# An fp32 encoder layer on one core: weight sums moved from GpSimd to VectorE at the seams, seven stores moved to GpSimd's queue, and the last output columns scaled ahead

## The chip, the cores and the metric

The kernel runs on one core of one Trainium2 chip. A core has a matrix engine (TensorE, PE in the profile), three engines for element work (VectorE or DVE, ScalarE or ACT, GpSimd or POOL), and SyncE (SP), which here only issues transfers; ACT and GpSimd can issue transfers as well. Each engine runs its own instructions in a fixed order and waits on semaphores for the others. On-chip memory is SBUF (128 partitions) and PSUM (where PE writes); the big tensors lie in device memory. The metric is device microseconds of the execution.

## The reference

Two groups of 512 tokens (prompt and sample, 1024 channels) pass through one layer with shared weights, everything in fp32. What matters here are the parts in which the change lies:

```python
y_m = (sigmoid(o) * hm) @ w_mo                      # mLSTM branch
y_a = mla_attention(...) @ w_ao                     # attention branch
x = x + (g_m * y_m + g_a * y_a) @ w_out
h2 = rmsnorm(x, g_ffn)
x = x + (silu(h2 @ w_gate) * (h2 @ w_up)) @ w_down  # 1024 -> 2816 -> 1024
x = x + sigmoid(x @ w_ple_gate) * (p_l @ w_ple)     # the embedding's rows
return rmsnorm(x, g_final)
```

The last norm divides each token by the root of its mean square over all 1024 channels, and multiplies each channel by its gain. So no output can be finished before the last channel of its tokens is known.

## The kernel before, in words

**Layout.** Activations lie as channels by tokens in tiles of 128x512 (one group's 512 tokens). `x2[g][c]` is the running sum x of group g and channel block c. Group 0 is written first; of group 1 the last two channel blocks are worked in two halves of 256 tokens.

**Three matmuls for one.** Every fp32 operand is split into a rounded part (hi) and a remainder (lo); a product is hi·hi, hi·lo and lo·hi (lines 947, 948 and 949: `xh,wp`, `xl,wp`, `xh,wp`). ACT makes the rounded part with a cast (line 896 for weights, 1229 or 880 for activations), DVE the remainder with a subtraction (line 154). So each weight tile costs ACT one cast and DVE one subtraction, and line 949 is the first matmul of a product that needs the remainder.

**Seven products for eight.** From `w_mo` on, the projections (`mo`, `ao`, then `fg` and `fu` for gate and up, then `down`) are done by a class `Seven`: two column blocks of weights and both token groups form a 2x2 block product, which is done in seven products (P1, P2, P7, P6, P5, Q4, P3) instead of eight. For that, four sums of weight blocks are formed, by `weights` (lines 922, 923, 925, 932: P7 two, P6 one, P3 one), all on GpSimd, and sums of activations, by `Ops.part` (858 P7, 861 P6, 864 P5, 867 Q4). The raw weights of a Seven come as two transfers of 512 KB (384 KB in the third part of down) that ACT issues (line 908), into tiles `wst`, which have two buffers in each of two pools, WP and WX. `outputs` copies PSUM results (982 on ACT, 987 on DVE), and `sg` (line 1199) multiplies gate by up.

**The stages.** `chain` strings the Sevens: mo 0 to 3, ao 0 to 3; then, after the output projection and a norm, eleven pairs of (fg, fu), then 3 x 4 Sevens of down, by parts of 4, 4 and 3 k-blocks. A pair takes the hidden blocks f1 and f2; its seven activation tiles (four products and three or four sums of them, lines 1204 to 1207) are stored to device memory (`actd`, line 1210) through SP's queue and loaded back by down (`ld`, line 828, on SP too). The last pair is the one with f2 = NF - 1; its tiles are read by down's third part only.

**The end.** `halves` loads the weights of the embedding's gate, `proj2` multiplies, and `embed` (DVE twice, ACT once) adds the gated embedding rows (`ld` from `emd`) to x; ACT squares the result (`sq`), DVE adds the squares, PE sums them over partitions (`ssc`), ten small DVE operations make the inverse root (`rv` to `rw`), PE spreads it over partitions (`rbc`), and `finish` multiplies x, gain and `rbc` (`o`, one DVE operation for each channel block) and stores (line 1319, SP). These last functions show as line 79 in the profile where they are called in a fixed order.

**What sets the order.** Up to the embedding's last columns a scheduler orders each engine's instructions by its own times for them. From `pinned[0] = True` on, the order of PE, DVE, ACT and GpSimd is the order of the code; SP's is not fixed by it.

## Time and profile before

| | |
|---|---|
| median of three runs | 1896.21 us (1896.04 to 1897.09) |
| the profiled execution | 1895.6 us |
| its span, first to last event | 1893.8 us |
| granted PE clock, mean | 0.991 |
| PE busy | 1848.4 us, 98% of the span |
| DVE busy | 1234.6 us, 65% |
| ACT busy | 883.3 us, 47% |
| GpSimd (POOL) busy | 448.7 us, 24% |

The profile's times are microseconds from the span's start. A timeline row gives start, duration, engine, line, operation, output and inputs, and in square brackets the idle time of the engine before it and what ended it. Rows of the same line that follow one another directly are drawn together (x2, x4); an operation's duration on DVE and ACT overlaps the start of the next by about 0.1 us, so a row of many shows the pitch. The waits view sums idle time by the pair "who waited for whom": us in total, times, longest.

### The profile page before, as it was taken

How to read it: one execution, taken by the hardware profiler on the slowest of the kernel's cores; microseconds unless marked ns; L12 is line 12 of the kernel's file. 1: busy time of each engine (PE TensorE's matmuls, PEld its weight loads, DVE VectorE, ACT ScalarE, POOL GpSimd, SP SyncE). 2: the span in 40 equal slices, each digit the busy share in tenths (PEclk: the TensorE clock that was granted, in tenths of full speed). 3: DMA queues.
4: the chain of work that ended last, by engine and by line, in shares of the span. 5: the costliest groups of instructions: out<-in, count | busy, mean ns of one | idle time of the engine just before them, and what ended most of it. 6: DMA issues, size and time to landing. Idle time of an engine off the chain costs nothing.

```text
span 1893.8 us, 24548 instructions
## 1 busy us (share of the span) xinstructions
PE 1848.4 (98%) x8849; PEld 1537.3 (81%) x8849; DVE 1234.6 (65%) x2159; ACT 883.3 (47%) x1718; POOL 448.7 (24%) x326
## 2 busy tenths in 40 slices
PE   9999999999999999999999998999999999999997
PEld 7888898988887888777877887888888887887886
DVE  6747575836555667975997586444444458878757
ACT  6255465534443666774543354333333344434442
POOL 0000000100000000352330035666466642322100
PEclk9999999999999999999999999999999999999999
DMA  4111101112253222446455241232323346534232
GB/s 165 52 45 35 56 34 62 40 56 73 78 182 116 65 73 93 126 150 209 153 191 192 95 161 51 91 131 92 103 89 111 112 146 228 165 126 135 90 124 89
DMA packets 98458, 207.59 MB, mean 110 GB/s; under 512 B 10721, under 2 KB 21345, under 8 KB 98337
## 3 DMA queue, kind: packets, MB, share of 16 engines
q1 hardware_dynamic: 86240, 163.03, 25.7%
q10 hardware_dynamic: 12096, 43.00, 7.0%
q8 instruction: 69, 1.13, 0.3%
q14 instruction: 53, 0.43, 0.1%
HBM read 151.89 MB, written 54.10 MB: 109 GB/s over the span
## 4 chain that ended last, share of the span: by engine, by line
PE 84%; DVE 9%; DMA 2%; ACT 2%; issue 2%; SPq 0%; DVEq 0%; ACTq 0%
PE b L947 12%; PE b L949 12%; PE b L948 12%; PE mm L183 8%; PE mm L185 8%; PE mm L184 8%; PE mm L79 4%; PE nm L633 3%; DVE xl L154 2%; PE mm L548 2%; PE mm L550 2%; PE mm L549 2%; DVE wp L154 1%; PE pt L812 1%; PE mm L1296 1%
## 5 line engine op out<-in xcount | busy, mean ns | idle before, releaser
L949 PE MATMUL b<-xh,wp 128*128 128x512 f32 x1148 | 445.1, 393 | 7.5 <-DVE wp L154 7.5
L947 PE MATMUL b<-xh,wp 128*128 128x512 f32 x1148 | 442.5, 394 | 9.4 <-ACT wp L896 3.9
L948 PE MATMUL b<-xl,wp 128*128 128x512 f32 x1148 | 448.9, 392 | 0.0
L896 ACT CAST wp<-wst 128x512 fp32r<-128x512 f32 (+1 forms) x270 | 164.5, 613 | 306.8 <-PE b L949 258.6
L154 DVE TENSOR_TENSOR wp<-wst,wp 128x512 fp32r<-128x512 f32 (+1 forms) x270 | 244.2, 907 | 75.2 <-ACT wp L896 74.9
L947 PEld LDWEIGHTS b<-xh,wp 128*128 128x128 f32 x1148 | 216.5, 189 | 63.0 <-ACT wp L896 8.4
L949 PEld LDWEIGHTS b<-xh,wp 128*128 128x128 f32 x1148 | 216.4, 188 | 56.0 <-DVE wp L154 8.8
L948 PEld LDWEIGHTS b<-xl,wp 128*128 128x128 f32 x1148 | 216.5, 189 | 46.7
L183 PE MATMUL mm<-hh,whi 128*128 128x512 f32 x560 | 220.0, 393 | 0.3 <-ACT raw L79 0.3
L185 PE MATMUL mm<-hh,wlo 128*128 128x512 f32 x560 | 219.5, 392 | 0.0
L184 PE MATMUL mm<-hl,whi 128*128 128x512 f32 x560 | 219.5, 392 | 0.0
L922 POOL TENSOR_TENSOR s<-wst,wst 128x512 f32<-128x512 f32 (+1 forms) x42 | 64.1, 1526 | 422.7 <-DMA wst<-w 268.8
L987 DVE TENSOR_TENSOR u<-b,u 128x512 f32<-128x512 f32 x90 | 61.6, 690 | 142.1 <-PE b L949 85.0
L168 ACT CAST whi<-wst 128x1024 fp32r<-128x1024 f32 (+1 forms) x69 | 71.1, 1030 | 116.5 <-PE mm L184 78.4
L183 PEld LDWEIGHTS mm<-hh,whi 128*128 128x128 f32 x560 | 105.6, 189 | 22.6 <-ACT raw L79 0.8
L185 PEld LDWEIGHTS mm<-hh,wlo 128*128 128x128 f32 x560 | 105.4, 188 | 21.9
L184 PEld LDWEIGHTS mm<-hl,whi 128*128 128x128 f32 x560 | 105.6, 189 | 21.5
L154 DVE TENSOR_TENSOR wlo<-wst,whi 128x1024 fp32r<-128x1024 f32 (+1 forms) x69 | 83.2, 1206 | 30.8 <-ACT whi L168 30.4
L154 DVE TENSOR_TENSOR xl<-ld,xh 128x512 fp32r<-128x512 f32 x121 | 94.1, 806 | 11.3 <-ACT xh L1229 5.9
L982 ACT COPY u<-b 128x512 f32<-128x512 f32 x90 | 50.9, 589 | 107.8 <-PE b L949 80.1
L154 POOL TENSOR_TENSOR vnl<-avt,vnh 128x512 fp32r<-128x512 f32 x16 | 21.2, 1323 | 313.5 <-ACT vnh L158 245.2
L925 POOL TENSOR_TENSOR wst<-wst,wst 128x512 f32<-128x512 f32 (+1 forms) x42 | 79.2, 1886 | 35.9 <-DVE wp L154 33.7
(348 smaller groups left out, 3634.7 us busy)
## 6 DMA issues: line engine op xcount, KB each, us to landing
wst<-w SPq DMA_DIRECT2D x73, 512.0 KB
wst<-w ACTq DMA_DIRECT2D x60, 512.0 KB
ld<-actd SPq DMA_DIRECT2D x77, 256.0 KB
actd<-t SPq DMA_DIRECT2D x44, 256.0 KB
actd<-sg SPq DMA_DIRECT2D x33, 256.0 KB
x<-x SPq DMA_DIRECT2D x32, 256.0 KB
ld<-hzd SPq DMA_DIRECT2D x32, 256.0 KB
wst<-wd ACTq DMA_DIRECT2D x16, 512.0 KB
```

The source lines that it names most:

```text
L79: r = f(*args, **kw)
L154: e.tensor_tensor(out=out, in0=src, in1=hi.bitcast(F32), op=ALU.subtract)
L168: S.copy(hi[:, :n], st[:, :n])
L183: E.matmul(bk, whi[:, c], hi, start=k == 0, stop=False)
L184: E.matmul(bk, whi[:, c], lo, start=False, stop=False)
L185: last_mm[0] = E.matmul(bk, wlo[:, c], hi, start=False, stop=k == nk - 1)
L896: S.copy(hi, src)
L922: GP.tensor_tensor(out=src, in0=a11, in1=a21, op=ALU.add)
L925: GP.tensor_tensor(out=a11, in0=a11, in1=a21, op=ALU.add)
L947: E.matmul(bk, whi[:, c], hi, start=bool(first) and k == 0, stop=False, **sk)
L948: E.matmul(bk, whi[:, c], lo, start=False, stop=False, **sk)
L949: E.matmul(bk, wlo[:, c], hi, start=False, stop=k == self.kh - 1, **sk)
```

## The change

Four edits. `Seven` takes the engine of its weight sums as an argument, and twelve Sevens are given VectorE: the last mo, the first ao, both Sevens of the first and of the last gate pair, and the first and the last of each part of down. That is 48 sums. The Q4 sums of the gate stage's activations (four, line 867) also go to VectorE. The seven stores of the last gate pair are issued by GpSimd; they are the only transfers that GpSimd issues in the program. The embedding's rows are loaded into tiles of the pool's tag `h` (24 buffers) instead of `ev` (8). And at the end the last half's columns of group 1 are multiplied by the gain on ACT ahead of the norm (`scaled`), into three tiles `xg` of the tag `wst` in WP, which has two buffers; DVE then multiplies four, two and two blocks at once by the spread inverse root (`last_out`), and three stores follow, of 512, 256 and 256 KB. The last embedding's step comes one step earlier.

```diff
-        def __init__(self, srcs, kh, ops, out):
+        def __init__(self, srcs, kh, ops, out, adds=None):
+            self.adds = adds or GP
...
-                GP.tensor_tensor(out=src, in0=a11, in1=a21, op=ALU.add)
-                GP.tensor_tensor(out=a21, in0=a21, in1=a22, op=ALU.add)
+                self.adds.tensor_tensor(out=src, in0=a11, in1=a21, op=ALU.add)
+                self.adds.tensor_tensor(out=a21, in0=a21, in1=a22, op=ALU.add)
...
     def pair(kind, c, ops, put):
+        e = V if (kind, c) in (("mo", 3), ("ao", 0)) else GP
...
-    h2 = Ops(hn, lambda: OP("ev", "t"), lambda n: GP if n == "Q4" else V)
+    h2 = Ops(hn, lambda: OP("ev", "t"), lambda n: V)
...
-                    nc.sync.dma_start(actd[f1, n], t_)
+                    (GP if f2 == NF - 1 else nc.sync).dma_start(actd[f1, n], t_)
...
         def make(kind, put):
+            e = V if f1 == 0 or f2 == NF - 1 else GP
...
+                lambda c=c: Seven(
+                    [a[f"wd{pi}"][c], a[f"wd{pi}"][c + 1]], nk, ld, add_to(c, c + 1), V if c in (0, KD - 2) else GP
+                ),
...
-        bp = load(emd[g][c], OP, "ev") if bp is None else bp
+        bp = load(emd[g][c], OP, "h") if bp is None else bp
...
+    def scaled(g, cs, b0, nb):
+        n = nb * P
+        xg = WP("wst", "xg", F32, (P, 1024))[:, 0 : len(cs) * n]
+        for i, c in enumerate(cs):
+            S.activation(
+                out=xg[:, i * n : (i + 1) * n], in_=x2[g][c][:, b0 * P : b0 * P + n], func=AF.Copy,
+                scale=col("g_final", c),
+            )
+        return xg
+
+    def last_out(g, cs, xg, b0, nb):
+        n, k = nb * P, len(cs)
+        tok = slice(b0 * P, b0 * P + n)
+        x3_ = xg.rearrange("p (c t) -> p c t", c=k)
+        V.tensor_tensor(out=x3_, in0=x3_, in1=rs2[g][:, None, :].to_broadcast([P, k, n]), op=ALU.mult)
+        nc.sync.dma_start(a[f"out{g}"][cs[0] : cs[0] + k][:, :, tok].rearrange("c p t -> p c t"), x3_)
...
     first = rs2[1]
+    embed(KD - 1, 1, bk[3], toks[1], bps[1], True)
+    gained = [(cs, scaled(1, cs, H0, H0)) for cs in (range(0, 4), range(4, 6), range(6, 8))]
     finish(1, [0, 1], 0, H0)
-    embed(KD - 1, 1, bk[3], toks[1], bps[1], True)
-    finish(1, [2, 3], 0, H0)
     sums(1, H0, H0)
     inv(1, H0)
-    finish(1, [4, 5], 0, H0)
+    finish(1, [2, 3], 0, H0)
     spread3(1, H0, H0)
     rs2[1], second = first, rs2[1]
-    finish(1, [6, 7], 0, H0)
+    finish(1, [4, 5, 6, 7], 0, H0)
     rs2[1] = second
-    finish(1, list(range(KD)), H0, H0)
+    for cs, xg in gained:
+        last_out(1, cs, xg, H0, H0)
```

How instructions move is shown at three places. Line numbers after the change are one higher from 923 on, two from about 1075 on.

**The start of the gate stage, on DVE.** `wp_11187` is the split weight of the second Seven's P7 (made from the sum `s_2084`), `t` are the activations' sums, `hn` the normed activations. Before, the rows up to it are:

```order
L864 TENSOR_TENSOR hn_10604<-hn_10604,hn_10900 128x512
L987 TENSOR_TENSOR u_11048<-b_2067_11057,u_11048 128x512
L154 TENSOR_TENSOR xl_10966<-t_10942,xh_10964 128x512
L154 TENSOR_TENSOR wp_11146<-wst_11030,wp_11146 128x512
L154 TENSOR_TENSOR xl_10997<-hn_10555,xh_10995 128x512
L154 TENSOR_TENSOR wp_11166<-wst_11030,wp_11166 128x512
L154 TENSOR_TENSOR xl_11002<-hn_10604,xh_11000 128x512
L987 TENSOR_TENSOR u_11089<-b_2073_11094,u_11089 128x512
L154 TENSOR_TENSOR xl_11007<-t_10924,xh_11005 128x512
L154 TENSOR_TENSOR wp_11187<-s_2084_11184,wp_11187 128x512
```

Of the change:

```order
L864 TENSOR_TENSOR hn_10604<-hn_10604,hn_10900 128x512
L867 TENSOR_TENSOR t_10930<-t_10930,hn_10488 128x512
L154 TENSOR_TENSOR wp_11166<-wst_11030,wp_11166 128x512
L154 TENSOR_TENSOR xl_10966<-t_10942,xh_10964 128x512
L154 TENSOR_TENSOR xl_10997<-hn_10555,xh_10995 128x512
L988 TENSOR_TENSOR u_11089<-b_2073_11094,u_11089 128x512
L154 TENSOR_TENSOR wp_11187<-s_2084_11184,wp_11187 128x512
L867 TENSOR_TENSOR t_10936<-t_10936,hn_10561 128x512
L154 TENSOR_TENSOR wp_11204<-wst_11028,wp_11204 128x512
L154 TENSOR_TENSOR xl_11002<-hn_10604,xh_11000 128x512
L867 TENSOR_TENSOR t_10942<-t_10942,hn_10610 128x512
L154 TENSOR_TENSOR xl_11007<-t_10924,xh_11005 128x512
```

Between the first weight split of the stage, `wp_11032`, and `wp_11187` there are 45 other rows on DVE before and 49 with the change: four weight sums and two Q4 sums have come in, two remainders (`xl_11002`, `xl_11007`) have gone behind. The first Sevens' other four weight sums stand on DVE ahead of `wp_11032`.

**The last gate pair's stores.** Before, on SP, they stand among the loads of down's first part:

```order
L1210 DMA actd_14349<-sg_14006 128x512
L828 DMA ld_14287<-actd_12226 128x512
L1210 DMA actd_14339<-sg_14066 128x512
L1210 DMA actd_14345<-t_14329 128x512
L1210 DMA actd_14341<-t_14330 128x512
L1210 DMA actd_14343<-t_14331 128x512
L828 DMA ld_14351<-actd_11370 128x512
L828 DMA ld_14357<-actd_11656 128x512
L828 DMA ld_14363<-actd_11942 128x512
L1210 DMA actd_14347<-t_14332 128x512
L828 DMA ld_14369<-actd_12228 128x512
```

With the change, on GpSimd:

```order
L1212 DMA actd_14337<-sg_13871 128x512
L923 TENSOR_TENSOR s_2678_14487<-wst_14375,wst_14377 128x512
L1212 DMA actd_14349<-sg_14006 128x512
L924 TENSOR_TENSOR wst_14377<-wst_14377 128x512
L926 TENSOR_TENSOR wst_14375<-wst_14375,wst_14377 128x512
L933 TENSOR_TENSOR wst_14375<-wst_14375 128x512
L1212 DMA actd_14339<-sg_14066 128x512
L1212 DMA actd_14345<-t_14329 128x512
L1212 DMA actd_14341<-t_14330 128x512
L1212 DMA actd_14343<-t_14331 128x512
L1212 DMA actd_14347<-t_14332 128x512
L923 TENSOR_TENSOR s_2691_14611<-wst_14523,wst_14525 128x512
```

SP's loads follow one another without a store, and GpSimd's stores stand around the weight sums of down's second Seven (`s_2678`) and ahead of the third's (`s_2691`). The buffers of three later loads on SP (`ld_14413`, `ld_14419`, `ld_14431`) come free when three of GpSimd's stores have landed.

**The end, on DVE and ACT.** Before, the last rows of DVE after the inverse root `rw_16930` are:

```order
L79 SCALAR_TENSOR_TENSOR o_16932<-x_1928_10549,cols,rbc_16892 128x256
L79 SCALAR_TENSOR_TENSOR o_16932<-x_1940_10598,cols,rbc_16892 128x256
L79 SCALAR_TENSOR_TENSOR o_16939<-x_1957_10658,cols,rbc_16892 128x256 [waits DMAHW6_49]
L79 SCALAR_TENSOR_TENSOR o_16939<-x_1960_10689,cols,rbc_16892 128x256
L79 SCALAR_TENSOR_TENSOR o_16943<-x_1871_10331,cols,rbc_16936 128x256 [waits DMAHW7_49,PE_49]
L79 SCALAR_TENSOR_TENSOR o_16943<-x_1886_10390,cols,rbc_16936 128x256
L79 SCALAR_TENSOR_TENSOR o_16947<-x_1892_10427,cols,rbc_16936 128x256
L79 SCALAR_TENSOR_TENSOR o_16947<-x_1904_10476,cols,rbc_16936 128x256
L79 SCALAR_TENSOR_TENSOR o_16951<-x_1928_10549,cols,rbc_16936 128x256
L79 SCALAR_TENSOR_TENSOR o_16951<-x_1940_10598,cols,rbc_16936 128x256
L79 SCALAR_TENSOR_TENSOR o_16955<-x_1957_10658,cols,rbc_16936 128x256 [waits DMAHW0_49]
L79 SCALAR_TENSOR_TENSOR o_16955<-x_1960_10689,cols,rbc_16936 128x256
```

With the change, after `rw_16937`:

```order
L79 SCALAR_TENSOR_TENSOR o_16939<-x_1892_10427,cols,rbc_16892 128x256 [waits DMAHW6_49]
L79 SCALAR_TENSOR_TENSOR o_16939<-x_1904_10476,cols,rbc_16892 128x256
L79 SCALAR_TENSOR_TENSOR o_16946<-x_1928_10549,cols,rbc_16892 128x256
L79 SCALAR_TENSOR_TENSOR o_16946<-x_1940_10598,cols,rbc_16892 128x256
L79 SCALAR_TENSOR_TENSOR o_16950<-x_1957_10658,cols,rbc_16892 128x256 [waits DMAHW7_49]
L79 SCALAR_TENSOR_TENSOR o_16950<-x_1960_10689,cols,rbc_16892 128x256
L79 TENSOR_TENSOR xg_16901<-xg_16901,rbc_16943 128x1024 [waits PE_49,Activation_49]
L79 TENSOR_TENSOR xg_16906<-xg_16906,rbc_16943 128x512 [waits Activation_49]
L79 TENSOR_TENSOR xg_16909<-xg_16909,rbc_16943 128x512 [waits DMAHW3_49,DVE_49,Activation_49]
```

And the last rows of ACT, which are new but for the first:

```order
L79 ACTIVATE sq_16899<-x_1960_10689 128x256 [waits DVE_49]
L79 ACTIVATE xg_16901<-x_1871_10331,cols 128x256
L79 ACTIVATE xg_16901<-x_1886_10390,cols 128x256
L79 ACTIVATE xg_16901<-x_1892_10427,cols 128x256
L79 ACTIVATE xg_16901<-x_1904_10476,cols 128x256
L79 ACTIVATE xg_16906<-x_1928_10549,cols 128x256 [waits Activation_49]
L79 ACTIVATE xg_16906<-x_1940_10598,cols 128x256
L79 ACTIVATE xg_16909<-x_1957_10658,cols 128x256 [waits DMAHW3_49,DVE_49]
L79 ACTIVATE xg_16909<-x_1960_10689,cols 128x256
```

The eight products `o` of the second half are replaced by eight gain scalings on ACT and three wide products on DVE. `xg_16909` lies in the buffer of `xg_16901`, and its first scaling waits for a transfer (`DMAHW3`), which is the store of `xg_16901`.

## The prediction

> **What bounds the kernel now.** I read the page first, then the waits of PE, then the timeline around each wait that the change touches.

> ```profile
> PE 1848.4 (98%) x8849; PEld 1537.3 (81%) x8849; DVE 1234.6 (65%) x2159; ACT 883.3 (47%) x1718; POOL 448.7 (24%) x326
> ```

> PE is busy for 1848.4 of 1893.8 us, and the change takes no matmul away. So all that can be won or lost is idle time of PE, 45.4 us, and it is worth asking only which pieces of it the four edits reach.

> ```profile
> PE b L949 <- DVE wp L154: 7.5, 3, 5.3
> PE b L947 <- ACT wp L896: 3.9, 4, 1.7
> PE b L947 <- DVE xl L154: 1.2, 1, 1.2
> ```

> Of the first row 5.3 us are one wait at the start of the gate stage and 1.95 one at the start of down; of the second, 1.74 are at the start of down too and 0.73 inside it; the 1.2 of the last row stand between mo and ao. The rows for these places follow with their parts. Together these three rows are 12.6 us, and with the tail, after the last big product, that is all that the change can reach.

> **The change part by part.**

> *Start of the gate stage.* PE first, then DVE, then GpSimd:

> ```profile
> 1150.26 0.50 PE L947 MATMUL b<-xh,wp 128*128 128x512 f32 x1 [0.19 <-ACT wp L896]
> 1156.34 0.79 PE L949 MATMUL b<-xh,wp 128*128 128x512 f32 x1 [5.34 <-DVE wp L154]
> ```

> ```profile
> 1109.29 0.69 DVE L79 TENSOR_TENSOR x<-x,mm 128x512 f32<-128x512 f32 x1 [2.33 <-PE mm L79]
> 1118.85 1.29 DVE L154 TENSOR_TENSOR wp<-wst,wp 128x512 fp32r<-128x512 f32 x2
> 1143.79 0.69 DVE L864 TENSOR_TENSOR hn<-hn,hn 128x512 f32<-128x512 f32 x1
> 1144.39 0.69 DVE L987 TENSOR_TENSOR u<-b,u 128x512 f32<-128x512 f32 x1
> 1146.11 1.78 DVE L154 TENSOR_TENSOR wp<-wst,wp 128x512 fp32r<-128x512 f32 x1
> 1154.54 1.75 DVE L154 TENSOR_TENSOR wp<-s,wp 128x512 fp32r<-128x512 f32 x1
> ```

> ```profile
> 1130.11 15.53 POOL L925 TENSOR_TENSOR wst<-wst,wst 128x512 f32<-128x512 f32 x1 [7.11 <-DVE wp L154]
> 1147.30 6.77 POOL L867 TENSOR_TENSOR t<-t,hn 128x512 f32<-128x512 f32 x4
> 1154.03 1.71 POOL L1199 TENSOR_TENSOR sg<-sg,u 128x512 f32<-128x512 f32 x1
> ```

> PE waits for the remainder `wp<-s` at 1154.54 (`wp_11187`). DVE reaches it late because from 1145 on each of its operations with two SBUF inputs takes 1.75 to 1.79 us where it took 0.69 (0.60 from start to start, as 1143.79 to 1144.39) before. That is exactly the stretch in which GpSimd runs its sums: one weight sum that could not get on from 1130 to 1145, one more, then the four Q4 sums (6.77 us). The two engines hold each other up in turn: GpSimd stands still while DVE runs such operations closely, then both crawl. The change takes all of these sums off GpSimd and puts them on DVE at 0.60 each.

> How long DVE then needs: 45 rows stand between the first `wp` at 1118.85 and `wp_11187` before, 49 after. So 50 x 0.60 = 30.0 us, from 1118.85 to about 1149, where before the start was at 1154.54. `wp_11187` is then done before 1150, and line 949 needs it at about 1151. The 5.34 us go as a whole; the 0.19 stay, since they hang on ACT's cast. The four early weight sums stand where DVE waits for the norm and has idle time (2.33 us before 1109.29), and cost nothing; without that cover they would cost 2.4.

> What is late next: behind `wp_11187` the two other Q4 sums and two remainders now stand (four rows, 2.4 us) ahead of the splits of the following products, and GpSimd still does `sg` (1154.03, 1.71) and the second pair's weight sums, each of which turns one or two DVE operations from 0.69 into about 1.77. PE now comes 5 us earlier to splits that were made in the shadow of its wait. A row of the windows by time (after the length: busy time of PE, weight loads, DVE, ACT and GpSimd):

> ```profile
> 1156.30:1200.00 43.70, 43.66 (x182) 35.67 (x183) 21.34 (x26) 14.51 (x25) 21.45 (x15) 0.95 0.28 97
> ```

> A product is 12 matmuls of 43.66/182 = 0.24 us, 2.9 us, and DVE has half of its time idle there. I take back 1.1 us (1.77 - 0.69) for one split that meets a sum on GpSimd, rounded up to 1.2. Gain **4.1**; bounds 5.3 (nothing comes late) and 2.8 (two or three splits do, 2.5 us).

> *Start of down.* SP's queue, then ACT:

> ```profile
> 1572.27 0.38 SPq L828 DMA_DIRECT2D ld<-actd  x1
> 1581.43 0.32 SPq L1210 DMA_DIRECT2D actd<-sg  x1
> 1582.64 2.72 SPq L1210 DMA_DIRECT2D actd<-t  x3
> 1585.45 1.49 SPq L828 DMA_DIRECT2D ld<-actd  x3
> 1587.47 8.46 SPq L828 DMA_DIRECT2D ld<-actd  x7
> ```

> ```profile
> 1589.19 0.62 ACT L1229 CAST xh<-ld 128x512 fp32r<-128x512 f32 x1 [1.89 <-DMA ld<-actd]
> 1592.87 0.62 ACT L1229 CAST xh<-ld 128x512 fp32r<-128x512 f32 x1 [3.06 <-DMA ld<-actd]
> 1593.39 0.61 ACT L896 CAST wp<-wst 128x512 fp32r<-128x512 f32 x1
> ```

> ```profile
> 1594.06 0.50 PE L947 MATMUL b<-xh,wp 128*128 128x512 f32 x1 [1.74 <-ACT wp L896]
> 1596.74 0.50 PE L949 MATMUL b<-xh,wp 128*128 128x512 f32 x1 [1.95 <-DVE wp L154]
> ```

> SP issues in order, and from 1572.7 to 1581.4 it stands before a store of the last pair whose `sg` does not exist yet; three more stores follow. So three loads of down go out only at 1585.45 to 1586.6; ACT waits for them 1.89 and 3.06 us, and the weight casts behind (the first at 1593.39) come late for PE: 1.74 + 1.95 = 3.7 us. With the stores on GpSimd the three loads wait for buffers alone, which DVE frees between about 1576 and 1581, so they go 5 to 9 us earlier, and the 3.7 us go with them, if the stores do no harm on GpSimd. GpSimd issues no transfer in the run before; there is no row for it. Queued behind them there are the four weight sums of down's second Seven and those of the third, and three loads on SP wait for the landing of three stores. Bounds: at best all 3.7. At worst a store holds GpSimd as long as one of its sums, 1.6 us (the rows of 1147.30, 6.77/4 = 1.7), so that three stores issued from 1582.6 on are out by 1587.5, and each transfer takes as long as the slowest here (third load issued at about 1586.1, waited for until 1592.87: 6.8): landed 1594.3, the loads behind them at 1601.1, split 1.2 later, 1602.3. Their product comes two products after the first one, that is at 1594.06 - 1.74 + 2 x 2.9 = 1598.1 without the waits: 4.2 lost against 3.7 won, -0.5. Halfway lies 1.6; I take **1.9**, nearer to the upper end, as DVE is not closely filled here and GpSimd gets its turns:

> ```profile
> 1575.00:1600.00 25.00, 21.32 (x89) 16.86 (x88) 20.20 (x27) 9.54 (x17) 9.27 (x7) 0.95 0.62 205
> ```

> *Weight sums on DVE elsewhere.* They come ahead of remainders in DVE's order, and a sum waits for its weights' transfer, which GpSimd could afford to do:

> ```profile
> 1545.91 0.33 ACTq L908 DMA_DIRECT2D wst<-wd  x1
> 1549.88 1.30 POOL L922 TENSOR_TENSOR s<-wst,wst 128x512 f32<-128x512 f32 x1 [2.85 <-DMA wst<-wd]
> 1549.30 0.69 DVE L154 TENSOR_TENSOR wp<-wst,wp 128x512 fp32r<-128x512 f32 x1
> ```

> At this place the first sum stands on DVE just ahead of the remainder of 1549.30: DVE would stand from 1549.3 to 1549.9, add for 1.2 us, and be 1.8 late for a product that starts at about 1551.6. I charge **-0.2** (0 to -0.5). In the other places of gate and down DVE has slack and GpSimd's 1.6 us a sum were hidden; removing them is worth nothing but for

> ```profile
> 1744.20 1.34 ACT L896 CAST wp<-wst 128x384 fp32r<-128x384 f32 x3 [5.15 <-DMA wst<-wd]
> 1744.76 0.50 PE L947 MATMUL b<-xh,wp 128*128 128x512 f32 x1 [0.73 <-ACT wp L896]
> ```

> where a transfer of weights is late; its buffers come free a little earlier without GpSimd's sums: **0.3** (0 to 0.7).

> *Between mo and ao* DVE is full:

> ```profile
> 928.00:960.00 32.00, 30.37 (x132) 24.21 (x130) 32.00 (x49) 17.53 (x32) 7.58 (x5) 1.00 0.63 197
> ```

> DVE (third figure) is busy for all 32 us. Of the eight sums moved there some four fall into this stretch, 2.4 us more on DVE, and as many GpSimd sums of about 1.1 us of hindrance each go. They cancel: **0** (-1.0 to 0.5).

> *The embedding's rows* keep nobody waiting before: in DVE's waits from 1785 us to the end only ACT and PE release it, no transfer. With 24 buffers in place of 8 the loads can only go earlier: 0.

> *The tail.*

> ```profile
> 1880.69 0.87 DVE L79 SCALAR_TENSOR_TENSOR o<-x,cols,rbc 128x256 f32<-128x256 f32 x2
> 1881.47 0.42 DVE L79 SCALAR_TENSOR_TENSOR pt<-pt,ld 128x256 f32<-128x256 f32 x1
> 1885.50 0.16 DVE L79 SCALAR_TENSOR_TENSOR rw<-rt,rx 128x4 f32<-128x4 f32 x1
> 1885.58 4.78 DVE L79 SCALAR_TENSOR_TENSOR o<-x,cols,rbc 128x256 f32<-128x256 f32 x12
> ```

> ```profile
> 1881.58 9.19 SPq L1319 DMA_DIRECT2D out<-o  x8
> 1882.38 0.42 ACT L79 ACTIVATE sq<-x 128x256 f32<-128x256 f32 x1 [1.80 <-DVE x L79]
> 1101.73 1.23 DVE L154 TENSOR_TENSOR wlo<-wst,whi 128x1024 fp32r<-128x1024 f32 x1
> ```

> Before, the last `o` ends at 1885.58 + 4.78 = 1890.36, and the span 3.44 us later. With the change the two `o` of 1880.69 no longer stand ahead of the last embedding, so its chain up to `rw` comes 0.78 us earlier, to 1884.9. Then six `o` at 0.39 ((4.78 - 0.47)/11) to 1887.2, and the wide products: 1.23 (the nearest row, 128x1024) to 1888.4, 0.60 to 1889.0, and the third would end at 1889.6, 0.75 us ahead of before. But its tile has the first one's buffer, and ACT may write the gain products there only when that store of 512 KB, issued at about 1888.4, has landed. The price of a landing: below, two `o` (2 x 0.39) end every 0.78 us and the stores of 256 KB keep that pace, so 512 KB is put at no less than 1.56; above, a 512 KB load took 1549.88 - 1545.91 = 3.97. I take the middle, 2.8: 1891.2. Two scalings on ACT (0.42 and 0.34) to 1892.0, the product 0.69 to 1892.7, and 3.44 to the end: 1896.1, **-2.3** (-1.1 to -3.5).

> **Sum.** 4.1 + 1.9 - 0.2 + 0.3 + 0 - 2.3 = 3.8 us off the profiled span of 1893.8. The profiled execution took 1895.6, 0.6 under the median; I take the difference to the median, 1896.2 - 3.8 = **1892.4 us**.

> **The rivals.**

> *The seams close fully.* Nothing comes late behind `wp_11187` (5.3), the stores are harmless (3.7), the store of the tail lands in 1.56 us (-1.1): 5.3 + 3.7 + 0.1 - 1.1 = 8.0, **1888.2**. For it speaks that DVE is busy for only 21.3 of the 43.7 us after 1156; against it, three good ends at once. Near it lies the case that the tail's wait is hidden or that the third tile is not held up by the store, -0.7 there and not +2.3: **1889.4**.

> *DVE becomes the bound of the gate stage's start.* DVE is closely filled from 1117 to 1159 already, and the change gives it more rows there. If GpSimd's remaining sums fall on it just then, four splits come 1.1 us late each and PE waits for all of them, 4.4, and the gain is 0.9 in place of 4.1: **1895.6**.

> *GpSimd's stores starve.* Place: start of down. The row of 15.53 us at 1130.11 shows how long GpSimd can stand when DVE runs two-input operations closely. If the first of the three stores is held up like that, they are out at 1582.6 + 15.5 + 5 = 1603, and even at 3.7 us a transfer (1589.19 less 1585.45) their loads are split at 1611.6, where 1598.1 was wanted: 13.5 lost, 3.7 won, -9.8 in place of 1.9. Sum 3.8 - 11.7 = -7.9, **1904.1**. It decides from the point at which down loses 1.9 instead of winning 1.9, that is a wait of 5.6 us: from there the kernel is slower than before. Against it: DVE's idle fifth at this place. [...]

> **How the numbers follow.** What a measurement of this kernel can tell from no change is about 0.2%, 3.8 us. My forecast, 1892.4, has 0.45; it stands on that edge, and I give 0.24 of it to faster and 0.21 to same. The closed seams have 0.18 and the harmless tail 0.06, both faster; DVE as the bound 0.22, same; the starved stores 0.09, slower. Faster 0.48, same 0.43, slower 0.09. The terms' ends all together give 1887.1 to 1898.9; eight times in ten I put it from 1888.5, short of the closed seams, to 1897.0, with the starved stores left out above.

> **What would show it.** PE's wait of 5.3 us for `wp<-s` gone, DVE at 0.69 up to it, and the sum of "b L949 <- DVE wp" down from 7.5 to 1 to 3. No wait of PE at the start of down (3.7 before), the three loads on SP 5 to 9 us earlier; the page's GpSimd queue with seven transfers, and what its sums wait for behind them. In the tail, ACT's `xg` waiting about 2 to 3 us for a transfer. I am wrong if new waits of DVE for `wst` transfers show up, if PE waits in down for `xl<-ld` behind GpSimd's stores, or if the tail's third tile does not wait.

## The result: 10.5 us faster, nearly three times the forecast

The changed kernel takes 1886.12 us in the median of four runs (1882.36 to 1886.97), before 1896.65 (1896.04 to 1900.57, four runs). The ratio is 0.9942, 95% interval 0.9929 to 0.9955. The forecast was 1892.4, and its range ended at 1888.5.

The page of the changed kernel and its waits of PE (us in total, times, longest):

```profile
PE 1843.9 (98%) x8849; PEld 1534.1 (81%) x8849; DVE 1240.2 (66%) x2206; ACT 884.6 (47%) x1726; POOL 371.7 (20%) x281
```

```profile
PE b L948 <- ACT wp L896: 1.2, 1, 1.2
PE b L948 <- DVE xl L154: 1.2, 1, 1.2
PE b L949 <- DVE xl L154: 0.9, 1, 0.9
PE b L950 <- DVE wp L154: 0.6, 2, 0.4
```

(Lines 948 to 950 are 947 to 949 of before.) The waits for `wp` on DVE are down from 7.5 to 0.6, those for `wp` on ACT from 3.9 to 1.2. And PE is busy for 1843.9 us in place of 1848.4, with the same 8849 matmuls: they have become shorter by 4.5 us in sum. That is the main part that the prediction did not have.

Both traces have 8849 matmuls, so the start of the n-th can be compared. The difference (changed less before) grows only at a few places; a second profiled execution of the changed kernel (e12, below) stands beside the first:

| place (time before) | forecast | first execution | e12 |
|---|---|---|---|
| attention, 760 to 870, no edit there | 0 | +2.1 | +0.1 |
| mo to ao, 900 to 1000 | 0 | 0.0 | +0.3 |
| start of the gate stage, 1130 to 1185 | -4.1 | -8.15 | -8.15 |
| last gate pair, 1546 | +0.2 | +0.5 | +0.4 |
| start of down, 1580 to 1606 | -1.9 | -4.4 | -4.3 |
| inside down, 1744 | -0.3 | -1.5 | -1.5 |
| from the last big product to the end | +2.3 | +2.5 | +2.5 |

**The start of the gate stage.** PE, then DVE of the changed kernel:

```profile
1152.55 0.50 PE L950 MATMUL b<-xh,wp 128*128 128x512 f32 x1 [0.39 <-DVE wp L154]
```

```profile
1145.19 0.68 DVE L988 TENSOR_TENSOR u<-b,u 128x512 f32<-128x512 f32 x1
1147.00 0.68 DVE L154 TENSOR_TENSOR wp<-wst,wp 128x512 fp32r<-128x512 f32 x1
1151.81 0.68 DVE L154 TENSOR_TENSOR wp<-s,wp 128x512 fp32r<-128x512 f32 x1
```

Up to `wp_11187` (the row of 1151.81) the operations on DVE that took 1.75 to 1.79 now take 0.68, and of PE's wait of 5.34 us 0.39 is left. What went with the wait stands in rows of before that the prediction had not looked at, the matmuls behind it:

```profile
1149.45 0.39 PE L948 MATMUL b<-xl,wp 128*128 128x512 f32 x1
1149.68 0.39 PE L949 MATMUL b<-xh,wp 128*128 128x512 f32 x1
1156.93 0.63 PE L947 MATMUL b<-xh,wp 128*128 128x512 f32 x1
1157.36 0.63 PE L948 MATMUL b<-xl,wp 128*128 128x512 f32 x1
1157.79 0.63 PE L949 MATMUL b<-xh,wp 128*128 128x512 f32 x1
```

Ahead of the wait a matmul takes 0.39 and the next starts 0.23 later; behind it, 0.63 and 0.43. The last of the slow matmuls starts at 1160.35. The windows from 1145 to 1165 say the same, before and changed (after the busy times stand the granted clock, the DMA share and GB/s):

```profile
1145.00:1165.00 20.00, 14.46 (x53) 11.06 (x52) 15.53 (x16) 8.37 (x14) 13.43 (x9) 0.83 0.19 66
```

```profile
1145.00:1165.00 20.00, 19.61 (x86) 15.83 (x85) 17.19 (x26) 11.05 (x19) 12.73 (x5) 1.00 0.19 66
```

The granted clock was 0.83 and is 1.00. Finer windows of before show where: four neighbouring ones of 3.41 us each, the first holding the start of the wait.

```profile
1150.61:1154.02 3.41, 0.39 (x2) 0.00 (x0) 3.41 (x4) 1.24 (x2) 3.41 (x3) 1.00 0.13 35
1154.02:1157.43 3.41, 1.09 (x3) 0.90 (x4) 3.41 (x5) 2.14 (x4) 1.72 (x2) 0.50 0.51 195
1157.43:1160.85 3.42, 3.42 (x10) 2.65 (x9) 1.86 (x4) 0.00 (x0) 0.00 (x0) 0.50 0.33 106
1160.85:1164.26 3.41, 3.41 (x16) 2.76 (x15) 0.69 (x1) 1.04 (x2) 2.15 (x2) 1.00 0.13 50
```

PE (first busy time) is idle for 3.02 and 2.32 us in the first two, and the second and third are granted half the clock (0.50). On the edges of these windows, see the last section.

**The start of down.** SP's queue, GpSimd's and the listing of DMA issues of the changed kernel (the last figure: us from issue to landing), and PE:

```profile
1555.71 40.31 SPq L828 DMA_DIRECT2D ld<-actd  x24
```

```profile
1576.83 0.56 POOL L1212 DMA_DIRECT2D actd<-sg  x1 [4.45 <-DVE sg L1201]
1582.23 0.54 POOL L1212 DMA_DIRECT2D actd<-t  x1 [1.26 <-DMA wst<-wd]
```

```profile
actd<-t POOLq DMA_DIRECT2D x4, 256.0 KB, 4.6
```

```profile
1595.12 0.50 PE L949 MATMUL b<-xl,wp 128*128 128x512 f32 x1 [0.87 <-DVE xl L154]
```

A store costs GpSimd about 0.55 us and lands after 4.6; SP issues loads only. The waits of 1.74 and 1.95 are gone, and one of 0.87 is new. Here too slow matmuls stood behind the waits of before, and are gone:

```profile
1597.77 1.05 PE L947 MATMUL b<-xh,wp 128*128 128x512 f32 x2
1598.62 0.63 PE L948 MATMUL b<-xl,wp 128*128 128x512 f32 x1
```

**The last gate pair.** DVE waits for a transfer as feared, and PE a little for DVE:

```profile
1543.90 0.69 DVE L923 TENSOR_TENSOR s<-wst,wst 128x512 f32<-128x512 f32 x1 [0.58 <-DMA wst<-wd]
1545.97 0.50 PE L950 MATMUL b<-xh,wp 128*128 128x512 f32 x1 [0.20 <-DVE wp L154]
```

**The tail**, on DVE, ACT and SP of the changed kernel:

```profile
1873.68 2.43 DVE L79 SCALAR_TENSOR_TENSOR o<-x,cols,rbc 128x256 f32<-128x256 f32 x6
1876.03 1.81 DVE L79 TENSOR_TENSOR xg<-xg,rbc 128x1024 f32<-128x1024 f32 x2
1881.28 0.69 DVE L79 TENSOR_TENSOR xg<-xg,rbc 128x512 f32<-128x512 f32 x1 [3.44 <-ACT xg L79]
```

```profile
1880.34 0.91 ACT L79 ACTIVATE xg<-x,cols 128x256 f32<-128x256 f32 x2 [7.05 <-DMA out<-xg]
```

```profile
1877.27 5.10 SPq L1348 DMA_DIRECT2D out<-xg  x3
```

The third tile waits for the first one's store: issued 1877.27, ACT free to write at 1880.34, 3.07 us. DVE stands for 3.44.

### The profile page after: what moved, and what is told of

Its sections match the earlier page's. It is cut to its first block, busy times and chain, and to the rows that moved or that the text cites. A ratio compares the mean times of both kernels' runs of the same rounds, so it can differ in the third digit from the quotient of the medians.

```text
span 1885.2 us, 24471 instructions
## 1 busy us (share of the span) xinstructions
PE 1843.9 (98%) x8849; PEld 1534.1 (81%) x8849; DVE 1240.2 (66%) x2206; ACT 884.6 (47%) x1726; POOL 371.7 (20%) x281
## 4 chain that ended last, share of the span: by engine, by line
PE 85%; DVE 9%; DMA 2%; ACT 2%; issue 1%; SPq 0%; ACTq 0%; DVEq 0%
PE b L948 12%; PE b L950 12%; PE b L949 12%; PE mm L185 8%; PE mm L183 8%; PE mm L184 8%; PE nm L633 3%; PE mm L79 3%; DVE xl L154 2%; PE mm L548 2%; PE mm L550 2%; PE mm L549 2%; DVE wp L154 1%; PE pt L812 1%; PE mm L1303 1%
## 5 line engine op out<-in xcount | busy, mean ns | idle before, releaser
L949 PE MATMUL b<-xl,wp 128*128 128x512 f32 x1148 | 447.5, 391 | 0.9 <-DVE xl L154 0.9
L896 ACT CAST wp<-wst 128x512 fp32r<-128x512 f32 (+1 forms) x270 | 164.1, 612 | 300.9 <-PE b L950 256.5
L154 DVE TENSOR_TENSOR wp<-wst,wp 128x512 fp32r<-128x512 f32 (+1 forms) x270 | 234.7, 871 | 67.0 <-ACT wp L896 66.9
L949 PEld LDWEIGHTS b<-xl,wp 128*128 128x128 f32 x1148 | 215.6, 188 | 47.9 <-DVE xl L154 1.5
L923 POOL TENSOR_TENSOR s<-wst,wst 128x512 f32<-128x512 f32 (+1 forms) x30 | 47.2, 1572 | 323.1 <-DMA wst<-wd 117.3
L154 DVE TENSOR_TENSOR wlo<-wst,whi 128x1024 fp32r<-128x1024 f32 (+1 forms) x69 | 83.3, 1207 | 31.2 <-ACT whi L168 30.6
L1201 POOL TENSOR_TENSOR sg<-sg,u 128x512 f32<-128x512 f32 x30 | 54.9, 1831 | 216.0 <-DVE u L988 216.0
L154 DVE TENSOR_TENSOR xl<-ld,xh 128x512 fp32r<-128x512 f32 x121 | 90.3, 773 | 6.2 <-ACT xh L880 5.2
L154 POOL TENSOR_TENSOR vnl<-avt,vnh 128x512 fp32r<-128x512 f32 x16 | 21.1, 1320 | 314.2 <-ACT vnh L158 245.9
```

The lines of the kernel that those rows point to most:

```text
L154: e.tensor_tensor(out=out, in0=src, in1=hi.bitcast(F32), op=ALU.subtract)
L896: S.copy(hi, src)
L949: E.matmul(bk, whi[:, c], lo, start=False, stop=False, **sk)
```

## The experiments

Theory A: a wait of PE costs its idle time and, from some length on, a stretch of matmuls at half speed behind it (0.43 us from start to start in place of 0.23, at a granted clock of 0.50, as in the rows above). Theory B: a wait costs its idle time alone, and the rest of the gain has other sources. The runs of before that stand beside these kernels had medians of 1896.75 (e1 to e4), 1895.59 (e5 to e8) and 1896.3 us (e9 to e12).

### e1: the first gate pair alone

```diff
 (on the kernel before)
-    h2 = Ops(hn, lambda: OP("ev", "t"), lambda n: GP if n == "Q4" else V)
+    h2 = Ops(hn, lambda: OP("ev", "t"), lambda n: V)
...
+            ... Seven(..., V if f1 == 0 else GP)
```

> The kernel before, with only the first gate pair's eight weight sums and the four Q4 sums on DVE. Theory A (a wait of PE costs its idle time and then some us of matmuls at half speed): about 7 to 8 us faster than before, 5.5 of them the wait and 2 to 2.5 the slow matmuls after it, which are gone with it. Theory B (a wait costs its idle time alone, and the rest of the gain came from elsewhere): 5 to 5.5 us faster, and matmuls of 0.63 us still stand near 1157.

1886.64 us (1885.17 to 1887.49), ratio 0.9946 (0.9928 to 0.9964). PE and the window:

```profile
1151.49 0.50 PE L950 MATMUL b<-xh,wp 128*128 128x512 f32 x1 [0.39 <-DVE wp L154]
```

```profile
1145.00:1165.00 20.00, 19.61 (x86) 15.80 (x86) 16.14 (x24) 10.17 (x17) 13.26 (x5) 1.00 0.19 66
```

PE gains 8.1 us at this place, 5.5 of idle time (5.34 + 0.19 + 0.35, a small wait at 1133, less 0.39) and 2.6 beyond it: some 2.1 of slow matmuls, the rest at the restarts (the first matmul behind a wait takes 0.50 in place of 0.39). Theory A. By these places the twelve sums are worth most of what the change gains.

### e2: the stores alone

```diff
 (on the kernel before)
-                    nc.sync.dma_start(actd[f1, n], t_)
+                    (GP if f2 == NF - 1 else nc.sync).dma_start(actd[f1, n], t_)
```

> The kernel before, with only the last gate pair's seven stores on GpSimd. Theory A: the 3.7 us of waits at the start of down and the 1.8 us of slow matmuls behind them go, less a new wait of about 1 for later loads: 4 to 5 us faster. Theory B: 2.5 to 3.5 us faster. If the gain there came from the weight sums on DVE and not from the queue: under 1 us.

1889.04 us (1888.4 to 1893.11), ratio 0.9963 (0.9947 to 0.9980). The window, the one wait of PE left at the place, and the stores:

```profile
1575.00:1595.00 20.00, 20.00 (x90) 16.47 (x89) 20.00 (x26) 8.47 (x15) 12.21 (x12) 1.00 0.79 269
```

```profile
1597.41 0.50 PE L948 MATMUL b<-xl,wp 128*128 128x512 f32 x1 [0.27 <-DVE xl L154]
```

```profile
actd<-t POOLq DMA_DIRECT2D x4, 256.0 KB, 4.1
```

PE gains 5.2 us at the start of down, 0.8 more than in the full change: 3.4 of idle time, 1.8 of slow matmuls and restarts. The queue makes this gain. DVE is busy for all 20 us here, and the stores land in 4.1 all the same: nothing starves.

### e3: another buffer for the third tile

```diff
 (on the changed kernel)
-        xg = WP("wst", "xg", F32, (P, 1024))[:, 0 : len(cs) * n]
+        xg = (WX if cs[0] == 6 else WP)("wst", "xg", F32, (P, 1024))[:, 0 : len(cs) * n]
```

> The changed kernel, with the third tile of the end taken from the other pool, so that nothing waits for the store of the first. The last product on DVE then follows at 1877.8 instead of 1881.3: 3.4 us less than the changed kernel, about 1882.7 us, 14 less than before. If the queue of stores sets the end and not that wait: within 1 us of the changed kernel.

1882.73 us (1880.55 to 1885.69), ratio 0.9930 (0.9916 to 0.9945). DVE, SP, and the GB/s of the span's last 13.8 us in 40 slices:

```profile
1873.05 2.40 DVE L79 TENSOR_TENSOR xg<-xg,rbc 128x1024 f32<-128x1024 f32 x3
```

```profile
1874.29 1.96 SPq L1348 DMA_DIRECT2D out<-xg  x3
```

```profile
GB/s 0 0 0 0 0 0 0 0 0 237 359 163 0 0 0 0 0 0 39 341 324 336 326 342 344 229 92 353 338 335 359 321 362 339 350 190 0 0 0 0
```

The wait is gone, and DVE follows without a break. But from the last big product to the end the kernel takes as long as before (0.0), where 0.75 less was worked out; the gain is 2.4 and not 3.4. From 1872.6 on the stores run at about 340 GB/s almost to the end, with one dip: I take it that their pace sets the end, and e8 is made to test that.

### e4: four waits put into PE's way

```diff
 (on the changed kernel, in proj2)
         bk = bank()[:, tok]
+        if steps:
+            V.tensor_copy(out=lag, in_=after[:, 0:4])       # waits for the last product
+            for _ in range(steps):
+                V.tensor_scalar(out=lag, in0=lag, scalar1=1.0, scalar2=None, op0=ALU.mult)
+            V.tensor_copy(out=bk[:, 0:4], in_=lag)          # PE's next product waits for this
```

> The changed kernel with four waits put into PE's way in the last stage, by chains of 2, 6, 16 and 11 small DVE operations between two products (some 1, 2, 4 and 3 us of idle time). Theory A: after the waits of 2 us and more the matmuls run at half speed for 3 to 5 us (0.63 us each instead of 0.39), so that each costs 1.5 to 2.5 us beyond its idle time, and the shortest nothing. Theory B (slow matmuls come from what else happens at the seams, contention or transfers): no slow matmuls behind any of the four.

1898.48 us in one run. PE's waits of 1.77, 3.81 and 2.79 us with rows behind each; the last has matmuls of 128x256, for which a row of the kernel before follows:

```profile
1847.08 0.47 PE L79 MATMUL mm<-xh,wp 128*128 128x512 f32 x1 [1.77 <-DVE mm L79]
1847.62 0.63 PE L79 MATMUL mm<-xh,wp 128*128 128x512 f32 x2
1856.61 0.47 PE L79 MATMUL mm<-xh,wp 128*128 128x512 f32 x1 [3.81 <-DVE mm L79]
1858.14 1.05 PE L79 MATMUL mm<-xh,wp 128*128 128x512 f32 x2
1859.00 0.63 PE L79 MATMUL mm<-xl,wp 128*128 128x512 f32 x1
1866.79 0.36 PE L79 MATMUL mm<-xh,wp 128*128 128x256 f32 x1 [2.79 <-DVE mm L79]
1867.87 0.63 PE L79 MATMUL mm<-xh,wp 128*128 128x256 f32 x2
```

```profile
1877.26 0.40 PE L79 MATMUL mm<-xh,wp 128*128 128x256 f32 x2
```

Two matmuls of 128x512 together take 0.63 in the fast stretches here and 1.05 in the slow one. So behind 1.77 there is nothing, behind 3.81 a slow stretch (1857.7 to 1860.9), behind 2.79 too (0.63 for two that take 0.40). Theory A, at a place where neither GpSimd nor a seam is near. The first chain ran beside other work, and PE waited there for ACT, 1.16 us, with nothing slow behind.

### e5 and e6: the two kinds of sums apart

```diff
 (e5, on the kernel before)
-    h2 = Ops(hn, lambda: OP("ev", "t"), lambda n: GP if n == "Q4" else V)
+    h2 = Ops(hn, lambda: OP("ev", "t"), lambda n: V)
 (e6, on the kernel before)
+            ... Seven(..., V if f1 == 0 else GP)
```

> The kernel before, with only the four Q4 sums of the gate stage on DVE; the first pair's weight sums stay on GpSimd. If the Q4 sums on GpSimd made most of the wait: DVE loses four hindrances of 1.1 us and gains two sums of 0.6 ahead of the split that PE waits for, so PE's wait of 5.3 us falls to about 2, at the edge where slow matmuls follow or not; PE's end of the stage 3 to 6 us earlier. If the weight sums made it: under 2 us earlier.

> The kernel before, with only the first pair's eight weight sums on DVE; the Q4 sums stay on GpSimd. If both kinds of sums are needed for the gain: PE's wait stays above 2.5 us and slow matmuls follow, 1 to 4 us gained of the 8.1. If the weight sum that stood on GpSimd from 1130 to 1145 was the cause, because the Q4 sums stood behind it: 7 to 8 us gained.

One run each, 1895.15 and 1893.72 us. e5, PE and GpSimd:

```profile
1156.01 0.50 PE L949 MATMUL b<-xh,wp 128*128 128x512 f32 x1 [3.30 <-DVE wp L154]
```

```profile
1132.28 16.14 POOL L925 TENSOR_TENSOR wst<-wst,wst 128x512 f32<-128x512 f32 x1 [7.12 <-DVE wp L154]
```

e6, the same:

```profile
1153.55 0.50 PE L950 MATMUL b<-xh,wp 128*128 128x512 f32 x1 [1.55 <-DVE wp L154]
```

```profile
1140.82 8.04 POOL L867 TENSOR_TENSOR t<-t,hn 128x512 f32<-128x512 f32 x3 [147.71 <-DVE xl L154]
```

PE gains 3.1 us at the place with the Q4 sums moved, 4.6 with the weight sums (the second includes 0.6 of the small wait at 1133), 8.1 with both. Each kind alone leaves a sum on GpSimd that meets DVE shortly before the split that PE waits for, and a wait with a slow stretch behind (from 1157.6 in e5, from 1153.9 in e6). Both are needed. The rows of before and of e5 also show when the long weight sum on GpSimd gets through: DVE runs operations with two SBUF inputs without a break (0.69 each before, 0.68 in e5), and the sum, which takes 15.53 us before and 16.14 in e5, ends in both 1.25 us after DVE starts its first one with a PSUM input (`u<-b,u`: 1144.39 and 1145.64 before, 1147.17 and 1148.42 in e5). That is about what one of GpSimd's sums takes elsewhere in the run before (1.30, at 1549.88).

### e7 and e8: what the late sums and the wide products are worth

```diff
 (e7, on e3)
-            e = V if f1 == 0 or f2 == NF - 1 else GP
+            e = V if f1 == 0 else GP
...
-                    ..., add_to(c, c + 1), V if c in (0, KD - 2) else GP
+                    ..., add_to(c, c + 1), GP
 (e8, on e3)
-    gained = [(cs, scaled(1, cs, H0, H0)) for cs in (range(0, 4), range(4, 6), range(6, 8))]
...
-    for cs, xg in gained:
-        last_out(1, cs, xg, H0, H0)
+    finish(1, list(range(KD)), H0, H0)
```

> The kernel of e3, with the weight sums of the last gate pair and of down back on GpSimd. Theory: these sums on DVE cost 0.5 us near 1546 (DVE waits for a transfer) and some 0.9 at the start of down (the new wait for xl), so both go; the 1.5 us gained inside down (near 1744) come back as a loss only if the sums made them. 1881 to 1883 us; in the trace -0.5 and -0.9 at the two places.

> The kernel of e3 with the last half's columns finished as before (eight products of x, gain and spread root, four stores of 256 KB), but with the last embedding's step one step earlier, as in the change. If the end is set by the stores' pace of about 340 GB/s: the same as e3 within 0.7 us. If the wide products on DVE are what shortens the end: 1 to 2 us slower than e3.

e7: 1881.86 us (1879.2 to 1883.39), ratio 0.9928 (0.9911 to 0.9946). Against e3 PE is 0.25 us earlier at the last gate pair, where it now loses nothing, and 0.6 at the start of down, where the wait for `xl` stays, with 0.76 us in place of 0.95; inside down, near 1744, it gains 1.1 instead of 1.5. And e3 has a wait that e7 does not have and the change has hardly (it loses 0.2 us there), in e11 it is 1.22:

```profile
1654.79 0.50 PE L948 MATMUL b<-xh,wp 128*128 128x512 f32 x1 [1.63 <-DVE x L1239]
```

So these 32 sums on DVE bring 0.4 at one place and cost 0.8 at two, and now and then over a microsecond at a third. e8: 1882.88 us (1882.54 to 1883.75), ratio 0.9937 (0.9918 to 0.9955), against 1882.73 of e3. Its DVE:

```profile
1872.14 5.57 DVE L79 SCALAR_TENSOR_TENSOR o<-x,cols,rbc 128x256 f32<-128x256 f32 x14
```

DVE works for 5.6 us behind the inverse root and not for 4.8 (e3: 1870.70 to 1875.45), and from the root (`rw`) to the end of the span it takes 8.8 us against 9.1 in e3. The wide products shorten DVE's work and not the end.

### e9 to e12: the parts that gained, a part undone, the change again

```diff
 (e9 is e7 with e8's edit; e10, on e9)
-        e = V if (kind, c) in (("mo", 3), ("ao", 0)) else GP
+        e = GP
 (e11, on the changed kernel)
-                    (GP if f2 == NF - 1 else nc.sync).dma_start(actd[f1, n], t_)
+                    nc.sync.dma_start(actd[f1, n], t_)
```

> The parts that gained, together: the first gate pair's and the Q4 sums on DVE, mo's and ao's as in the change, the seven stores on GpSimd, the last embedding's step earlier; not the sums of the last gate pair and of down, and not the premultiplied columns. 1880 to 1882.5 us, 4 to 6 less than the change and about 14 less than before. If the sums in down or the wide products were worth something that e7 and e8 did not show: 1883 or more.

> The kernel of e9, with the sums of mo and ao back on GpSimd too. If these cancel, as the prediction said (0): the same as e9 within 0.5 us, and no difference of PE's starts between 900 and 1000. If they gained what DVE was held up there: 1 to 2 us slower.

> The changed kernel with the last pair's stores back on SP. If the queue alone made the gain at the start of down: waits of PE of 3 to 4 us there again, with slow matmuls behind, 4 to 5 us lost against the changed kernel up to 1600. If the weight sums on DVE had a part: 2 to 3 us.

> The changed kernel once more, on the same chip as e9 and e10, for their difference: 1885 to 1887 us.

| kernel | median us (lowest to highest) | ratio to before (95%) |
|---|---|---|
| e9 | 1881.59 (1879.82 to 1882.25) | 0.9920 (0.9906 to 0.9933) |
| e10 | 1880.54 (1878.85 to 1884.87) | 0.9921 (0.9908 to 0.9933) |
| e11 | 1890.82, one run | |
| e12, the change | 1885.80 (1885.34 to 1886.42) | 0.9946 (0.9932 to 0.9960) |

e10 is the smallest version: twelve sums on DVE, seven stores on GpSimd, the rows of the embedding in other tiles, the last embedding's step earlier. It is some 5 us faster than the whole change; between e9 and e10 no difference can be told, nor in PE's starts between 900 and 1000 (no shift of 0.05 us in either): the sums of mo and ao cancel, as forecast. In e11 the waits come back, longer than before, and the slow matmuls with them:

```profile
1586.12 0.50 PE L948 MATMUL b<-xh,wp 128*128 128x512 f32 x1 [2.71 <-ACT wp L896]
1588.78 0.80 PE L950 MATMUL b<-xh,wp 128*128 128x512 f32 x1 [1.92 <-DVE wp L154]
```

Up to 1606 PE loses 2.1 us there and the full change wins 4.4: the stores are worth 6.5 with the other edits in place.

## Why the prediction was wrong

The direction was right, and so were most mechanisms; two terms of the sum were mis-sized by the same omission, and a third effect was put at nothing for a reason that does not hold.

**Start of the gate stage: 4.1 forecast, 8.15 measured.** The step that failed is "The 5.34 us go as a whole" as the whole price of that wait. The wait had a second part, ten matmuls at half speed, 2.1 us, and 0.5 at the restarts. The row of 1156.34 itself showed it: 0.79, where the first matmul behind the other waits takes 0.50. Theory A, borne out by e1 and e4. The 1.2 us that I took back for splits coming late did not occur: DVE, free of GpSimd's sums, had `wp_11187` 0.39 late and the next ones in time. The reckoning of DVE's rows (50 at 0.60, about 30 us) was right: `wp_11187` ran at 1151.81, of which 2.3 belong to the later start of this execution.

**Start of down: 1.9 forecast, 4.4 measured** (5.2 in e2). Again the slow matmuls behind the waits, 1.6 us (1.8 in e2) with the restarts, were missing. And the middle value between the bounds was too cautious about GpSimd: an issue took 0.55 us, not up to 1.7, and the landing 4.1 to 4.6, not 6.8. The starved stores did not occur, even in e2 with DVE full.

**Inside down: 0.3 forecast, 1.5 measured.** The sum took this from the weight sums, and put the embedding's rows at 0, as "the loads can only go earlier". That step failed: five of the eight went later. SP before and with the change:

```profile
1729.35 9.31 SPq L828 DMA_DIRECT2D ld<-emd  x8
1719.22 6.63 SPq L828 DMA_DIRECT2D ld<-emd  x3
```

In the five kernels without that edit (before, e1, e2, e5, e6) eight of these loads go out just ahead of and between the two transfers of weights for this product; in the nine with it three do, ahead of both, and the next one goes out more than 50 us later. In the 8 us up to the product the DMA engines were busy for 79% before (1736 to 1744, 258 GB/s) and are for 43% now (1726 to 1734, 131 GB/s), and in all nine kernels both waits of PE there (0.73 and 0.24 before) are gone. So the weights no longer share the way with the embedding's rows; no run makes this edit alone. Some 0.4 of the 1.5 hangs on down's sums (1.1 in e7, e9 and e10). And e1 gains 0.7 with the eight loads in place; why, no run shows.

**The last gate pair: -0.2 forecast, -0.5 and -0.4 measured**, by the wait described. **Between mo and ao: 0, as forecast.** **The tail: -2.3 forecast, -2.5 measured**: the store of 512 KB released its buffer after 3.07 us, where 2.8 was estimated; that it came so near is partly luck, as 2.8 was the middle between 1.56 and 3.97. There one step was still wrong: without that wait the end would not have come 0.75 us earlier, since the stores' pace of about 340 GB/s sets it by e3 and e8 (from `rw` to the end 9.1 and 8.8 us, with DVE at work for 4.8 and 5.6).

**The sum.** With the measured terms the change is worth 8.15 + 4.4 + 1.5 - 0.5 - 2.5 = 11.1 us, where my sum had 3.8. The two profiled executions differ by 8.6 only, because the first one of the changed kernel lost 2.1 us in the attention stage, which e12 did not; by medians it is 10.5. The rival "the seams close fully" came nearest, 1888.2: it had the seams' idle time nearly right, but no price for the slow matmuls, and of its three good ends the tail's did not come: the store took 3.07 us and not 1.56.

## What to carry to other kernels

Price a wait of PE by the matmuls behind it as well as by its idle time: look at their durations in the timeline and at the granted clock of a window around the wait. The waits of 5.34 and of 1.74 and 1.95 us cost 1.6 to 2.6 us more here, so closing these two seams paid half as much again as their idle time. Where two engines hold each other up with their sums (here 1.75 us in place of 0.69 on DVE, and 15.53 for one sum on GpSimd), give both kinds of sums to one of them, since half of it left a wait in place (3.1 and 4.6 of 8.1); when a tile moves to other buffers, look at when its loads now go out, and what they share the way with; and before shortening the last operations, check whether it is the stores behind them that set the end, as here at about 340 GB/s.

## What the runs showed of the hardware that was not expected

So where the grid lies decides. In the attention stage PE has the same wait for `apl` in both traces, 1.97 us before and 1.96 with the change: before, 1.63 of it fall into one window (from 809.27) and nothing slow follows; with the change all of it lies in one (from 810.15), and the next is at half the clock. 1.74 in a window of its own was not followed by slow matmuls (before, 1594), 1.77 was not either (e4, 1847), 0.55 and 1.55 within 2.84 us were (e6, from 1153.9). A wait of 3.9 us, twice 1.95, would by that always be followed by them, wherever the grid lies; this is an estimate from the 1.95 us above. At 420 there is no wait, but 24 matmuls of two columns in 2.6 us, and a window at half the clock follows in both traces. At a granted clock of 0.50 a window costs up to half its 3.41 us, 1.7 us (its matmuls start 0.43 us apart in place of 0.23); this too is an estimate. The times of the kernel before go with its mean clock: of its 28 executions that stand beside e1 to e12, the four with a mean clock of 0.994 took 1892.3 to 1894.1 us, the two with 0.989 took 1899.1 and 1901.6.
